# Neighbourhood attention scores: from two stacked full-array products per head to three half-row products for two heads at once

## The chip, the cores and the metric

The kernel runs on one core of one Trainium2 chip. The metric is the device time of one execution in microseconds (us). The core has four engines that compute: TensorE (PE, matrix products into PSUM, with weight loads that overlap the products), VectorE (DVE), ScalarE (ACT) and GpSimd (POOL). SyncE (SP) issues the DMAs. They run side by side, each through its own instructions in order, and wait for one another on semaphores.

## The reference, cut to what matters

One encoder layer over two requests of 2048 tokens with 1024 features. A normalised input is projected; four of the projections (q_b, k_b, v_b, g_b, each 512 wide) feed the second branch, an attention over a grid of 32 rows by 64 columns with 8 heads of 64 features. A token sees a window of 8 rows by 16 columns:

```python
def neighbourhood_attn(q, k, v, rpb):
    ...
    def row(r):
        ...
        kb = kr[:, :, key_cols]
        vb = vr[:, :, key_cols]
        sc = jnp.einsum('bnqhd,banchd->bnhqac', qr, kb).astype(jnp.float32) * scale
        ...
        sc = jnp.where(mask, sc + bias.astype(jnp.float32), -jnp.inf)
        sc = sc.reshape(b, NA_N_COL_BLOCKS, B_HEADS, NA_COL_BLOCK, wr * NA_KEY_COLS)
        pr = jax.nn.softmax(sc, axis=-1)
        ...
        o = jnp.einsum('bnhqac,banchd->bnqhd', pr, vb)
        return o.reshape(b, GRID_W, B_WIDTH)
```

q_b and k_b are normalised per head before this; the branch's output is multiplied by a gate and goes, with that of a first branch (windowed attention), through an output projection. All of it is in 32-bit floats.

## The kernel before, in words

**Precision.** PE's fast 32-bit form keeps fewer digits than a full float. So each operand is split into a high part, which is the value rounded to that form, and a low part, the rest, and a product is made of three: high by high, low by high, high by low. ACT writes the high part (a copy that rounds), DVE or POOL the low part (a subtraction).

**Stages.** A first stage handles the windowed attention, a second the neighbourhood attention, a third the output projection and what follows. In the second stage (loop at the end of `emit`, `f` from 2 x NT to 6 x NT) there are 64 units: two halves of four heads each, two requests, and sixteen blocks of 8 x 16 tokens. A unit is `unit_b(f)`. Its 128 queries meet a window of keys of 288, 360, 384 or 512 columns, by the block's place on the grid (`window`, L31).

**The order on PE is written out by hand.** Each product goes through `mm` (L201) or `tr` (L204, a transpose), and `pinned` (L193) chains them in the order of the program. The generator `stream` yields the projection products of tiles that come up to six units later (`proj_b`, 48 products of 512 columns per unit: `pqk` for queries and keys, `pvg` for values and gate). `PLAN_B` (L83) tells where in a unit's 10320 planned nanoseconds of projection each step of the attention is put in: `sc` (scores), `pt` (transposed weights of the softmax), `po` (product with the values), `fin` (gate and store), `prep` (the next unit's queries). An entry is the place, whether it belongs to this unit (1) or the previous one (0), the step and its index.

**The scores of one head before.** A head has 64 features, and PE has 128 rows. `keys_b` (L598) therefore stacks a head's keys: for the head at rows 0 to 63 of the transposed tile the high part lies in rows 0 to 63 and the low part in rows 64 to 127; for the other head it is the other way round. That takes, for each unit's key tile, four instructions of ACT (L607) and four of DVE (L608), each over 64 partitions. `prep_b` (L671) does the like for the queries: ACT writes the high part to one half (L680), DVE the low part to the same half of a second tile (L681) whose other half is zero, and POOL copies the high part to the other half (L683). With that, a head's scores are two products over all 128 rows (L713): the doubled high query by the stacked keys gives high by high and high by low at once, and the low query by the stacked keys gives low by high.

**After the products** `softmax` (L214, the instruction of L217) has DVE add the bias, take the maximum and free the PSUM buffer. Score buffers, the buffers of `pt` and that of `fin` share one tag, `sc`, with three PSUM buffers in turn (`PSB`, L60).

Of the kernel before, what the change touches and what calls it, by code (L numbers as in the profile page):

```python
# [11 lines left out]
F32 = mybir.dt.float32  # L12
F32R = mybir.dt.float32r
I32 = mybir.dt.int32
AF = mybir.ActivationFunctionType
ALU = mybir.AluOpType
# [22 lines left out]
def row_type(b):  # L39
    return (0, 1, 1, 2)[b]  # L40


def col_type(cb):
    return (0, 1, 1, 2)[cb]


def bias_offsets():
# [33 lines left out]
    (0.75, 1, "pt", 0), (0.79, 1, "pt", 1), (0.88, 1, "pt", 2),  # L81
)
PLAN_B = (  # L83
    (0.00, 1, "sc", 0), (0.03, 1, "sc", 1), (0.07, 1, "sc", 2), (0.09, 0, "po", 2), (0.11, 1, "sc", 3), (0.16, 0, "po", 3),
    (0.24, 0, "fin", 0), (0.35, 1, "prep", 0),
    (0.45, 1, "pt", 0), (0.52, 1, "pt", 1), (0.60, 1, "pt", 2), (0.66, 1, "po", 0), (0.74, 1, "pt", 3), (0.80, 1, "po", 1),
)
# [2 lines left out]
def emit(ctx, tc, io):  # L90
    nc = tc.nc
# [4 lines left out]
    def ptile(shape, tag, name):  # L96
        tag = PSM.get(tag, tag)
        return pp.tile(shape, F32, tag=tag, name=name, bufs=PSB[tag])
# [10 lines left out]
    wk = cp.tile([128, 2], F32, tag="wk", name="wk")  # L109
# [91 lines left out]
    def mm(out, lhsT, rhs, start, stop):  # L201
        pinned(nc.tensor.matmul(out, lhsT, rhs, start=start, stop=stop))  # L202

    def tr(out, in_):  # L204
        pinned(nc.tensor.transpose(out, in_, ident))  # L205
# [8 lines left out]
    def softmax(i, ps, n, bias, sm):  # L214

        s = main.tile([128, 512], F32, tag="s", name="s", bufs=SB)
        nc.vector.tensor_tensor_reduce(out=s[:, :n], in0=ps[:, :n], in1=bias, scale=1.0, scalar=-3.0e38,  # L217
                                       op0=ALU.add, op1=ALU.max, accum_out=sm["mx"][:, i:i + 1])
        sm["s"].append(s)
# [41 lines left out]
    ap = ab_stack.enter_context(tc.tile_pool(name="ab", bufs=1))  # L261
# [55 lines left out]
    def big(shape, dt, name):  # L317
        return ap.tile(shape, dt, tag="big", name=name, bufs=3)
# [38 lines left out]
    for i in range(4):  # L357
        nc.vector.tensor_tensor(out=tab[i // 2][:, i % 2], in0=cs[:, i % 2],
                                in1=rw[:, i].unsqueeze(1).broadcast_to([128, NT, 16]), op=ALU.mult)
# [4 lines left out]
    q2s = []  # L364
# [5 lines left out]
    ks_b, w_b, held = [], {}, {}  # L370
# [227 lines left out]
    def keys_b(kt, b, cb):  # L598
        pkt = ptile([128, 2, 16, 8], "ms", "pktb")
        for i in range(2):  # L600
            tr(pkt[:, i].rearrange("p c r -> p (c r)"), kt[:, 2 * i:2 * i + 2, :].rearrange("p h d -> p (h d)"))
        for i in range(2):
            for e in range(2):
                a, z = 64 * e, 64 - 64 * e
                hi, lo = (ks_b[i][p:p + 64, 8 * b:8 * b + 8, e, 16 * cb:16 * cb + 16].rearrange("p r c -> p c r")
                          for p in (a, z))
                nc.scalar.activation(hi, pkt[a:a + 64, i], AF.Copy, scale=wk[a:a + 64, 1:2])  # L607
                nc.vector.scalar_tensor_tensor(out=lo, in0=pkt[a:a + 64, i], scalar=wk[a:a + 64, 1:2],  # L608
                                               in1=hi.bitcast(F32), op0=ALU.mult, op1=ALU.subtract)

    def proj_b(f):
        half, st = divmod(f - 2 * NT, 2 * NT)
        s, j = divmod(st, NT)
        b, cb = divmod(j, 4)
        if f < 2 * NT + 8:
            regroup_next()
        if not ks_b:
            ks_b.extend(big([128, 32, 2, 64], F32R, f"ks_b{i}") for i in range(2))
        w_qk, w_vg = w_b[half]
        xr = xt.pop(f)  # L620
        pk = ptile([128, 512], "pj", "pqk")
        for i, c in enumerate(project(pk, xr, lambda k, b: ready("wa", k, w_qk)[:, b, :], 215)):
            at = i + 24 if f in last else i
            if i == PD and f == 2 * NT + 9:
                stats_b(1)
            if at in HX:
                split(f + 1, HX[at])
            yield c
        sq = ap.tile([128, 512], F32, tag="sq", name="sqb", bufs=2)
        nc.scalar.activation(sq, pk, AF.Square)  # L630
        ssq = ap.tile([128, 8], F32, tag="ssq", name="ssqb", bufs=3)
        nc.vector.tensor_reduce(out=ssq, in_=sq.rearrange("p (h d) -> p h d", d=HD), op=ALU.add, axis=AX.X)
        vr = ap.tile([128, 8], F32, tag="vr", name="vrb", bufs=2)
        y = ap.tile([128, 8], F32, tag="y", name="yb", bufs=4)
        nc.vector.tensor_scalar(out=vr, in0=ssq, scalar1=1.0 / HD, scalar2=ep_b[:, st:st + 1],
                                op0=ALU.mult, op1=ALU.add)
        rsqrt(ap, vr, y, 8, "rqb")
        qg = ap.tile([128, 2, 4, HD], F32, tag="qg", name="qg", bufs=6)
        kt = ap.tile([128, 4, HD], F32, tag="kt", name="kb", bufs=2)
        for dst, c in ((kt, 4), (qg[:, 0], 0)):  # L640
            nc.vector.tensor_tensor(out=dst, in0=pk[:, 64 * c:64 * c + 256].rearrange("p (h d) -> p h d", d=HD),
                                    in1=y[:, c:c + 4].unsqueeze(2).broadcast_to([128, 4, HD]), op=ALU.mult)
        yield 0, False
        pv = ptile([128, 512], "pj", "pvg")
        for i, c in enumerate(project(pv, xr, lambda k, b: ready("wb", k, w_vg)[:, b, :], 215)):
            if i + 24 in HX and f not in last:
                split(f + 1, HX[i + 24])
            yield c
            if i == (KB if f not in last else 10):
                if f < 2 * NT + 2:  # L650
                    pending.append((kt, b, cb))
                else:
                    keys_b(kt, b, cb)
        v = ap.tile([128, 4, 2, HD], F32R, tag="sq", name="vb", bufs=2)
        vp = pv[:, 0:256].rearrange("p (h d) -> p h d", d=HD)
        nc.scalar.activation(v[:, :, 0, :], vp, AF.Copy, scale=rs_b[:, st:st + 1])
        nc.vector.scalar_tensor_tensor(out=v[:, :, 1, :], in0=vp, scalar=rs_b[:, st:st + 1],
                                       in1=v[:, :, 0, :].bitcast(F32), op0=ALU.mult, op1=ALU.subtract)
        for w, (c0, ncol) in COL_WIN.items():
            lo, hi = max(c0, 16 * cb), min(c0 + ncol, 16 * cb + 16)  # L660
            if lo < hi:
                nc.sync.dma_start(v_d[half, s, w][8 * b:8 * b + 8, lo - c0:hi - c0].rearrange("r c h a d -> c r (h a d)"),
                                  v[8 * (lo - 16 * cb):8 * (hi - 16 * cb)].bitcast(F32).rearrange("p h a d -> p (h a d)"))
        gs = qg[:, 1].rearrange("p h d -> p (h d)")
        nc.scalar.activation(gs, pv[:, 256:512], AF.Tanh, scale=hr_b[:, st:st + 1])
        nc.vector.scalar_tensor_tensor(out=gs, in0=gs, scalar=1.0, in1=pv[:, 256:512], op0=ALU.add, op1=ALU.mult)
        held[f] = qg[:, 0], gs
        next(combining, None)
        yield 0, False

    def prep_b(f):  # L671
        q = held[f][0]
        pqt = ptile([128, 256], "ms", "pqtb")
        for i in range(2):
            tr(pqt[:, 128 * i:128 * i + 128], q[:, 2 * i:2 * i + 2, :].rearrange("p h d -> p (h d)"))
        q1 = ap.tile([128, 2, 256], F32R, tag="q1", name="q1b", bufs=3)
        q1, q2 = [q1[:, e] for e in range(2)], [q2s[f % 2][:, e, :256] for e in range(2)]
        for e in range(2):
            a, z = 64 * e, 64 - 64 * e
            nc.scalar.copy(q1[e][a:a + 64], pqt[a:a + 64])  # L680
            nc.vector.tensor_tensor(out=q2[e][a:a + 64], in0=pqt[a:a + 64], in1=q1[e][a:a + 64].bitcast(F32),  # L681
                                    op=ALU.subtract)
            nc.gpsimd.tensor_copy(q1[e][z:z + 64], q1[e][a:a + 64])  # L683
        return q1, q2

    bt = []

    def unit_b(f):
        half, st = divmod(f - 2 * NT, 2 * NT)
        s, j = divmod(st, NT)  # L690
        b, cb = divmod(j, 4)
        _, gs = held[f]
        r0, nr, c0, ncol, rows = window(b, cb)
        kc, nch = rows * ncol, nr // rows
        n = nr * ncol
        if cb != 2:
            off, _ = BIAS_OFF[(row_type(b), col_type(cb))]
# [4 lines left out]
        bias = bt[-1]  # L702
# [4 lines left out]
                              .rearrange("r c h a d -> (r c) (h a d)"))  # L707
        sm, p_ts, got = sm_tiles(), [], {}

        def sc(h):  # L710
            ps = ptile([128, 512], "sc", "scb")
            for j, q in enumerate(qs[f]):
                mm(ps[:, :n].rearrange("p (r c) -> p r c", c=ncol), q[h % 2][:, 128 * (h // 2):128 * (h // 2) + 128],  # L713
                   ks_b[h // 2][:, r0:r0 + nr, h % 2, c0:c0 + ncol], j == 0, j == 1)
            softmax(h, ps, n, bias[:, h, :n], sm)
            if h == 3:
                next(exps(sm, n, hr_b[:, st:st + 1], gs))

        def pt(x):
# [119 lines left out]
    qs = {}  # L839
# [85 lines left out]
    with tc.tile_pool(name="c", bufs=1) as op:  # L925
# [192 lines left out]
        for m in range(7 * len(groups)):  # L1118
            n, i = divmod(m, 7)
# [104 lines left out]
```

## Time and profile before

| what | us |
|---|---|
| median of 3 runs | 2605.88 |
| lowest and highest of them | 2604.47, 2607.68 |
| the profiled execution's own time | 2603.58 |
| its span, first to last instruction | 2601.7 |
| span of the second stage's scores, first to last product | 852 to 1888 |

The span is 1.9 us shorter than the execution's time; the rest lies around it. A row of a group reads: line of the kernel, engine, operation, tile written <- tiles read, shapes, count | busy time, mean ns of one | idle time of the engine before them, and what ended it. A row of a stretch reads: from : to, length, then busy time and count for PE, PEld (weight loads), DVE, ACT and POOL, the granted clock, the DMA engines' share and GB/s. A row of the waits reads: who waited for whom, us in total, times, longest. A row of the timeline reads: start, length, engine, line, operation, tiles, shapes, count.

### The profile page before, as it was taken

The page shows a single profiled execution, that of the slowest core. Times are in us where ns is not written, and L with a number is a line of the kernel's source. Part 1 is how long each engine was busy: PE and PEld are TensorE (multiplying, and loading weights), DVE is VectorE, ACT ScalarE, POOL GpSimd, SP SyncE. Part 2 cuts the span into 40 slices and gives each one's busy share as a digit, 9 for nine tenths or more (in the row PEclk, how much of TensorE's full clock was granted, in tenths as well). Part 3 has the DMA queues.
Part 4 walks back from the last instruction along what each step waited for, and adds up shares of the span by engine and source line. Part 5 has one row for each costly group of instructions (what it writes and reads, how often), then busy time and mean ns, then how long its engine had stood idle before and what let it go on. Part 6 is the DMA issues. An engine that isn't in the chain of part 4 may idle for free.

```text
span 2601.7 us, 47013 instructions
## 1 busy us (share of the span) xinstructions
PE 2547.1 (98%) x16080; PEld 2269.7 (87%) x16080; DVE 1963.3 (75%) x5702; ACT 1416.3 (54%) x3327; POOL 789.2 (30%) x996
## 2 busy tenths in 40 slices
PE   7999999999999999999999999999989999999999
PEld 6888888888877888888788888887989999999999
DVE  6888988889897788888888888888655648555454
ACT  5666666666675666666766666666432214222222
POOL 3333333333322333333233332321122423233321
PEclk9999999999999999999999999999999999999999
DMA  5333322111143564555654554457575445232221
GB/s 178 108 102 108 101 93 94 54 60 56 58 111 120 174 188 153 185 184 163 225 178 150 187 177 150 153 155 214 172 251 190 150 165 196 82 116 92 78 82 45
DMA packets 227519, 357.51 MB, mean 137 GB/s; under 512 B 37936, under 2 KB 115376, under 8 KB 222128
## 3 DMA queue, kind: packets, MB, share of 16 engines
q1 hardware_dynamic: 227280, 354.50, 42.8%
q8 instruction: 128, 2.10, 0.3%
q14 instruction: 111, 0.91, 0.1%
HBM read 266.33 MB, written 105.92 MB: 143 GB/s over the span
## 4 chain that ended last, share of the span: by engine, by line
PE 87%; DVE 5%; DMA 2%; ACT 2%; issue 2%; POOL 1%; SPq 0%; POOLq 0%; DVEq 0%; ACTq 0%
PE pqk L202 13%; PE pvg L202 12%; PE acca L1034 11%; PE accc L1034 9%; PE pg L202 6%; PE pq L202 5%; PE pob L202 4%; PE pple L202 3%; PE ptb L205 3%; PE scb L202 3%; PE pt L205 3%; PE po L202 3%; PE sc L202 3%; PE pk L202 3%; PE pout L202 3%
## 5 line engine op out<-in xcount | busy, mean ns | idle before, releaser
L232 ACT ACTIVATE s<-s,nm 128x384 f32<-128x384 f32 (+4 forms) x512 | 306.2, 599 | 340.6 <-DVE nm L228 185.0
L202 PE MATMUL pvg<-wb,xr 128*128 128x512 f32 x1536 | 455.2, 404 | 0.0
L202 PE MATMUL pqk<-wa,xr 128*128 128x512 f32 x1536 | 437.4, 407 | 0.0
L295 POOL TENSOR_TENSOR xr<-stx,xr 128x512 fp32r<-128x512 f32 x192 | 247.6, 1297 | 193.4 <-ACT xr L294 189.9
L202 PEld LDWEIGHTS pqk<-wa,xr 128*128 128x128 f32 x1536 | 267.5, 189 | 37.2
L202 PEld LDWEIGHTS pvg<-wb,xr 128*128 128x128 f32 x1536 | 267.4, 189 | 31.3
L202 PE MATMUL pg<-wb,xr 128*128 128x512 f32 x768 | 232.4, 410 | 4.1 <-DVE q L454 4.1
L202 PE MATMUL pq<-wa,xr 128*128 128x512 f32 x768 | 222.8, 404 | 3.6 <-ACT wa L147 2.8
L243 POOL TENSOR_TENSOR g<-qg,rd 128x256 f32<-128x256 f32 x64 | 39.7, 620 | 495.1 <-DVE rd L241 481.3
L1034 PE MATMUL acca<-opd,s 128*128 128x256 f32 x1344 | 164.6, 283 | 2.9 <-ACT r L1066 2.5
L1034 PEld LDWEIGHTS acca<-opd,s 128*128 128x128 f32 x1344 | 162.7, 192 | 3.6 <-ACT r L1066 2.7
L202 PEld LDWEIGHTS pq<-wa,xr 128*128 128x128 f32 x768 | 141.1, 191 | 28.3 <-ACT wa L147 3.4
L217 DVE CUSTOM_DVE_ANT_0 s<-scb,bias 128x288 f32<-128x288 f32 (+3 forms) x256 | 142.0, 555 | 29.1 <-PE scb L202 23.6
L202 PEld LDWEIGHTS pg<-wb,xr 128*128 128x128 f32 x768 | 137.9, 190 | 25.0 <-issue 4.6
L726 ACT CAST p_t<-ptb 96x384 fp32r<-96x384 f32 (+3 forms) x256 | 129.7, 508 | 54.1 <-PE ptb L205 52.3
L727 DVE TENSOR_TENSOR p_t<-ptb,p_t 96x384 fp32r<-96x384 f32 (+3 forms) x256 | 149.0, 584 | 9.1 <-ACT p_t L726 6.4
L607 ACT ACTIVATE ks_b<-pktb,wk 64x128 fp32r<-64x128 f32 x256 | 125.4, 490 | 49.1 <-DVE ks_b L608 40.6
L202 PEld LDWEIGHTS pob<-p_t,vw 128*128 128x128 f32 (+2 forms) x832 | 133.2, 190 | 20.8 <-DVE p_t L727 2.5
L608 DVE SCALAR_TENSOR_TENSOR ks_b<-pktb,wk,ks_b 64x128 fp32r<-64x128 f32 x256 | 115.1, 449 | 39.8 <-ACT ks_b L607 33.4
L202 PE MATMUL pob<-p_t,vw 128*128 128x256 f32 (+2 forms) x832 | 141.0, 283 | 2.0 <-DVE p_t L727 2.0
L1000 POOL TENSOR_TENSOR opd<-sum,opd 128x1024 fp32r<-128x1024 f32 x28 | 69.5, 2484 | 232.6 <-ACT opd L986 232.6
L217 DVE CUSTOM_DVE_ANT_0 s<-sc,mask 128x384 f32<-128x384 f32 (+1 forms) x256 | 135.8, 532 | 0.8
(197 smaller groups left out, 5909.1 us busy)
## 6 DMA issues: line engine op xcount, KB each, us to landing
stx<-x_b SPq DMA_DIRECT2D x128, 256.0 KB
vw<-v_d SPq DMA_DIRECT2D x112, 256.0 KB
stx<-x_a SPq DMA_DIRECT2D x64, 256.0 KB
stn<-x_n SPq DMA_DIRECT2D x64, 256.0 KB
v_d<-vb SPq DMA_DIRECT2D x64, 256.0 KB
x1r<-x_d SPq DMA_DIRECT2D x16, 1024.0 KB
y_t<-r SPq DMA_DIRECT2D x64, 256.0 KB
v_d<-vb SPq DMA_DIRECT2D x96, 128.0 KB
```

Source lines behind the costliest of these rows:

```text
L202: pinned(nc.tensor.matmul(out, lhsT, rhs, start=start, stop=stop))
L205: pinned(nc.tensor.transpose(out, in_, ident))
L217: nc.vector.tensor_tensor_reduce(out=s[:, :n], in0=ps[:, :n], in1=bias, scale=1.0, scalar=-3.0e38, op0=ALU.add, op1=ALU.max, accum_out=sm[ ...
L232: nc.scalar.activation(ss[i][:, :n], ss[i][:, :n], AF.Exp, bias=nm[:, i:i + 1], accum_out=den[:, i:i + 1])
L243: nc.gpsimd.tensor_tensor(out=g2, in0=gs.rearrange("p (h d) -> p h d", h=4), in1=rd.unsqueeze(2).broadcast_to([128, 4, HD]), op=ALU.mult)
L295: nc.gpsimd.tensor_tensor(out=lo, in0=raw, in1=hi.bitcast(F32), op=ALU.subtract)
L607: nc.scalar.activation(hi, pkt[a:a + 64, i], AF.Copy, scale=wk[a:a + 64, 1:2])
L608: nc.vector.scalar_tensor_tensor(out=lo, in0=pkt[a:a + 64, i], scalar=wk[a:a + 64, 1:2], in1=hi.bitcast(F32), op0=ALU.mult, op1=ALU.subtract)
L726: nc.scalar.copy(p_t[:kc, :nch, 0], pf)
L727: nc.vector.tensor_tensor(out=p_t[:kc, :nch, 1], in0=pf, in1=p_t[:kc, :nch, 0].bitcast(F32), op=ALU.subtract)
L1000: each(lambda x, y, z: eng.tensor_tensor(out=x, in0=y, in1=z, op=ALU.subtract), out, a, b)
L1034: pinned(nc.tensor.matmul(ps[:, kk], w[k][:, a, c:c + 128], o[:, b, k], start=i in (0, 1, 4) and kk == 0 and k == 0 and j == 0, stop=k == ...
```

## The change

Keys: `ks_b[0]` now holds the high part and `ks_b[1]` the low part of all four heads, head pair by head pair, each over all 128 partitions, so that a key tile takes two instructions of ACT and two of DVE. Queries: one tile with the high and the low part, one instruction of ACT and one of DVE, no copy on POOL. Scores: `sc(i)` handles heads 2i and 2i + 1 in two score buffers, with three products each. Head 2i uses partitions 0 to 63 of keys and queries, head 2i + 1 partitions 64 to 127, and the six products alternate between the two. The plan has two `sc` entries instead of four, at 0.00 and 0.10, and the previous unit's third `po` moves from 0.09 to 0.06. The products are the same three parts as before: high by high, low by high, high by low.

```diff
 PLAN_B = (
-    (0.00, 1, "sc", 0), (0.03, 1, "sc", 1), (0.07, 1, "sc", 2), (0.09, 0, "po", 2), (0.11, 1, "sc", 3), (0.16, 0, "po", 3),
+    (0.00, 1, "sc", 0), (0.06, 0, "po", 2), (0.10, 1, "sc", 1), (0.16, 0, "po", 3),
     (0.24, 0, "fin", 0), (0.35, 1, "prep", 0),
...
         for i in range(2):
-            for e in range(2):
-                a, z = 64 * e, 64 - 64 * e
-                hi, lo = (ks_b[i][p:p + 64, 8 * b:8 * b + 8, e, 16 * cb:16 * cb + 16].rearrange("p r c -> p c r")
-                          for p in (a, z))
-                nc.scalar.activation(hi, pkt[a:a + 64, i], AF.Copy, scale=wk[a:a + 64, 1:2])
-                nc.vector.scalar_tensor_tensor(out=lo, in0=pkt[a:a + 64, i], scalar=wk[a:a + 64, 1:2],
-                                               in1=hi.bitcast(F32), op0=ALU.mult, op1=ALU.subtract)
+            hi, lo = (k[:, i, 8 * b:8 * b + 8, 16 * cb:16 * cb + 16].rearrange("p r c -> p c r") for k in ks_b)
+            nc.scalar.activation(hi, pkt[:, i], AF.Copy, scale=wk[:, 1:2])
+            nc.vector.scalar_tensor_tensor(out=lo, in0=pkt[:, i], scalar=wk[:, 1:2], in1=hi.bitcast(F32),
+                                           op0=ALU.mult, op1=ALU.subtract)
...
-            ks_b.extend(big([128, 32, 2, 64], F32R, f"ks_b{i}") for i in range(2))
+            ks_b.extend(big([128, 2, 32, 64], F32R, f"ks_b{i}") for i in range(2))
...
-        q1 = ap.tile([128, 2, 256], F32R, tag="q1", name="q1b", bufs=3)
-        q1, q2 = [q1[:, e] for e in range(2)], [q2s[f % 2][:, e, :256] for e in range(2)]
-        for e in range(2):
-            a, z = 64 * e, 64 - 64 * e
-            nc.scalar.copy(q1[e][a:a + 64], pqt[a:a + 64])
-            nc.vector.tensor_tensor(out=q2[e][a:a + 64], in0=pqt[a:a + 64], in1=q1[e][a:a + 64].bitcast(F32),
-                                    op=ALU.subtract)
-            nc.gpsimd.tensor_copy(q1[e][z:z + 64], q1[e][a:a + 64])
-        return q1, q2
+        q = ap.tile([128, 2, 256], F32R, tag="q1", name="q1b", bufs=3)
+        nc.scalar.copy(q[:, 0], pqt)
+        nc.vector.tensor_tensor(out=q[:, 1], in0=pqt, in1=q[:, 0].bitcast(F32), op=ALU.subtract)
+        return q
...
-        def sc(h):
-            ps = ptile([128, 512], "sc", "scb")
-            for j, q in enumerate(qs[f]):
-                mm(ps[:, :n].rearrange("p (r c) -> p r c", c=ncol), q[h % 2][:, 128 * (h // 2):128 * (h // 2) + 128],
-                   ks_b[h // 2][:, r0:r0 + nr, h % 2, c0:c0 + ncol], j == 0, j == 1)
-            softmax(h, ps, n, bias[:, h, :n], sm)
-            if h == 3:
+        def sc(i):
+
+            pss = [ptile([128, 512], "sc", "scb") for _ in range(2)]
+            q = qs[f]
+            for j, (a, b) in enumerate(((0, 0), (1, 0), (0, 1))):
+                for e in range(2):
+                    r = slice(64 * e, 64 * e + 64)
+                    mm(pss[e][:, :n].rearrange("p (r c) -> p r c", c=ncol), q[r, a, 128 * i:128 * i + 128],
+                       ks_b[b][r, i, r0:r0 + nr, c0:c0 + ncol], j == 0, j == 2)
+            for e in range(2):
+                softmax(2 * i + e, pss[e], n, bias[:, 2 * i + e, :n], sm)
+            if i == 1:
                 next(exps(sm, n, hr_b[:, st:st + 1], gs))
```

## The prediction

> **What bounds the kernel now.** I read the first and fourth parts of the page first: what is busy, and which work the end hangs on.
>
> ```profile
> span 2601.7 us, 47013 instructions
> PE 2547.1 (98%) x16080; PEld 2269.7 (87%) x16080; DVE 1963.3 (75%) x5702; ACT 1416.3 (54%) x3327; POOL 789.2 (30%) x996
> ...
> PE 87%; DVE 5%; DMA 2%; ACT 2%; issue 2%; POOL 1%; SPq 0%; POOLq 0%; DVEq 0%; ACTq 0%
> ```
>
> TensorE (PE) is busy nearly all the time and carries 87% of the chain that ends last. The change touches the second attention stage alone, so the second look is the table of stretches for that stage (from the first product of its scores, 852 us, to the last, 1888 us) and the waits of PE within it.
>
> ```profile
> 852.00:1890.00 1038.00, 1026.41 (x5783) 875.75 (x5782) 838.22 (x2559) 664.46 (x1576) 315.40 (x391) 0.99 0.56 176
> ```
>
> ```profile
> PE pout L202 <- DVE o_r L802: 4.5, 3, 3.5
> PE ptb L205 <- ACT s L232: 2.4, 3, 1.0
> PE pob L202 <- DVE p_t L727: 2.0, 1, 2.0
> PE scb L202 <- DVE mx L217: 1.0, 1, 1.0
> PE scb L202 <- ACT qg L665: 1.0, 2, 0.5
> PE pktb L205 <- DVE otb L746: 0.3, 1, 0.3
> ```
>
> Of 1038 us PE is busy in 1026 at a granted clock of 0.99, and all its waits together are 11.2 us. VectorE (DVE) is busy in 838, ScalarE (ACT) in 664, GpSimd (POOL) in 315. In this stage the price of anything is what it does to PE; work taken from the others can win no more than some of those 11.2 us.
>
> **What the scores cost now.** Here are all their products, grouped by width (two kinds: the stacked high part q1b, and the low part q):
>
> ```profile
> L202 PE MATMUL scb<-ks_b,q1b 128*128 128x512 f32 x64 | 25.7, 402 | 2.0 <-DVE mx L217 1.0 <-ACT qg L665 1.0
> L202 PE MATMUL scb<-ks_b,q 128*128 128x512 f32 x64 | 25.5, 399 | 0.0
> ...
> L202 PE MATMUL scb<-ks_b,q 128*128 128x384 f32 x64 | 21.8, 341 | 0.0
> L202 PE MATMUL scb<-ks_b,q1b 128*128 128x384 f32 x64 | 21.7, 340 | 0.0
> L202 PE MATMUL scb<-ks_b,q 128*128 128x360 f32 x64 | 20.9, 326 | 0.0
> L202 PE MATMUL scb<-ks_b,q1b 128*128 128x360 f32 x64 | 20.8, 324 | 0.0
> ...
> L202 PE MATMUL scb<-ks_b,q1b 128*128 128x288 f32 x64 | 19.0, 296 | 0.1
> L202 PE MATMUL scb<-ks_b,q 128*128 128x288 f32 x64 | 18.9, 295 | 0.0
> ```
>
> Their mean durations overlap, so they aren't what a product takes of PE. That is the step from one start to the next, which the timeline gives:
>
> ```profile
> 1409.32 0.34 PE L202 MATMUL scb<-ks_b,q1b 128*128 128x384 f32 x1
> 1409.49 0.34 PE L202 MATMUL scb<-ks_b,q 128*128 128x384 f32 x1
> 1409.67 0.62 PE L202 MATMUL pvg<-wb,xr 128*128 128x512 f32 x2
> 1410.13 0.34 PE L202 MATMUL scb<-ks_b,q1b 128*128 128x384 f32 x1
> ```
>
> Two products of 384 columns take 0.35 us, two of 512 take 0.46 us: 0.458 and 0.449 ns a column. I take 0.455. A width has 128 products, so the scores stream 128 x (512 + 384 + 360 + 288) = 197,632 columns, 89.9 us.
>
> The same rows give the **tail**: the record of a 384-column product is 0.34 us, its step 0.175, so it runs 0.165 us on beside the next product.
>
> **Part 1, three half-row products for a pair of heads instead of four full ones.** A unit (64 of them) had four heads with two products each over 128 rows. Now a call handles two heads with three products each, one head on rows 0 to 63 and the other on rows 64 to 127, issued in turn: 128 calls of six. If the two halves really run together, a call takes three widths where two heads took four: 3/4 of 89.9 is 67.4 us, **-22.5 us**. No row of this trace has a 64-row product, so I bound it from the other side: if they run one after the other, there are six widths for four, 134.9 us, +45.0. I take the pair as concurrent: the halves share no row, weight or PSUM bank.
>
> The Trainium skill, "TensorE: Matmul & The Clock Gate", Part 3, says that matmuls on distinct row groups run concurrently and start about 4 ns apart; no run here shows it yet.
>
> **Part 2, the weight loads.** Loads rise from 8 to 12 a unit, each still 128 columns, two to a slot. How fast may load and product follow each other? The densest rows are transposes and 256-column products:
>
> ```profile
> 1403.54 0.49 PE L205 MATMUL ptb<-ident,s 128*128 128x128 f32 x3
> 1403.79 0.94 PE L202 MATMUL pqk<-wa,xr 128*128 128x512 f32 x3
> 1404.56 0.52 PE L202 MATMUL pob<-p_t,vw 128*128 128x256 f32 x3
> 1404.92 0.40 PE L202 MATMUL pqk<-wa,xr 128*128 128x512 f32 x1
> ```
>
> Three transposes and three 512-column products take 1.02 us; less 3 x 0.23 that is 0.11 for a transpose with its load. Three 256-column ones take 0.36, 0.12 each. Ends: the loads are hidden (0), or each couple of load and product costs its 0.11 and a slot can't be under 0.22. In the latter case 96 slots each of 384, 360 and 288 take 0.22 and 96 of 512 take 0.233: 85.7 us, and of the gain 4 us are left. I take 0: the loads of the 288-column products in the list above, step 0.13, leave no gap.
>
> **Part 3, changing between whole rows and half rows.** Every other product of the stage uses the whole array, so each call changes over and back: 256 changes. The low end is 0: in the rows just quoted transposes and products alternate, and the sum leaves nothing for it; nor do products with fewer rows show a gap:
>
> ```profile
> L202 PE MATMUL pob<-p_t,vw 96*128 96x256 f32 x192 | 32.9, 280 | 0.0
> ```
>
> But all of these start at row 0, one at a time. The new ones start at rows 0 and 64 and leave the array side by side. If the array has to empty first, the tail of the product before, 0.165 us, is no longer beside the next one; if the next weights may not be loaded meanwhile either, 0.11 comes on top, 0.275. I take 0.165, because the nearest thing to a half-row product waiting for the array is a product whose tail lies beside nothing: 256 x 0.165 = **+42.2 us**. Ends 0 and 70.4. The break-even is 22.5 / 256 = 0.088 us a change.
>
> The Trainium skill, "TensorEngine Tiling (Array Packing)", Key Properties, states that changing the tiling mode, not just the tile, drains the engine. It gives no price; by it the upper half of this interval is the place to look, and the trace, which has no such change, neither agrees nor disagrees.
>
> **Part 4, the splits.** Keys:
>
> ```profile
> L607 ACT ACTIVATE ks_b<-pktb,wk 64x128 fp32r<-64x128 f32 x256 | 125.4, 490 | 49.1 <-DVE ks_b L608 40.6
> ...
> L608 DVE SCALAR_TENSOR_TENSOR ks_b<-pktb,wk,ks_b 64x128 fp32r<-64x128 f32 x256 | 115.1, 449 | 39.8 <-ACT ks_b L607 33.4
> ```
>
> and queries:
>
> ```profile
> L680 ACT CAST q1b<-pqtb x128: 346/368/372, 801.0 to 1879.1; 64x256 fp32r<-64x256 f32 x128
> L683 POOL CAST q1b<-q1b x128: 392/394/801, 801.7 to 1879.8; 64x256 fp32r<-64x256 f32 x128
> L681 DVE TENSOR_TENSOR q<-pqtb,q1b x128: 405/422/431, 801.9 to 1880.3; 64x256 fp32r<-64x256 f32 x128
> ```
>
> Each pair over 64 partitions becomes one over 128 with as many elements a partition, so I give it the same duration. ACT loses 128 x 0.490 + 64 x 0.368 = 86 us, DVE 128 x 0.449 + 64 x 0.422 = 84 us, POOL its 128 copies of 0.394, 50 us. None of them is on the path: the six waits above name neither line. Gain 0, at most the waits on DVE and ACT, 6.7 us without `pout`. If a full-height split were twice as long, the engines would be where they are now: 0 too. No DMA is added or moved.
>
> **Part 5, order and buffers.** Heads 0 and 1 now come at the unit's start, heads 2 and 3 at 0.10 of it (1032 planned ns), with the previous unit's third `po` between, at 0.06. The three score buffers must now give two at once; the fourth head takes the buffer of the first, as before. It is free when DVE has read it:
>
> ```profile
> 1409.87 0.56 DVE L217 CUSTOM_DVE_ANT_0 s<-scb,bias 128x384 f32<-128x384 f32 x1
> ...
> 1410.36 0.68 DVE L632 TENSOR_REDUCE ssqb<-sqb 128x8 f32<-128x512 f32 x1
> ```
>
> From the product's end (1409.67) that is 0.76 us, or 1.44 with the 0.68 us reduction ahead of it. Between the calls PE has five projection products and a `po` of three: 5 x 0.23 + 0.36 = 1.5 us. So it just fits: 0. If another instruction like that reduction comes ahead, the second call waits 0.62 us, and with it everything on PE, since its order is fixed: 64 x 0.62 = 40 us.
>
> **Sum.** -22.5 + 42.2 = +19.7 us on the profiled execution's own 2603.6 us, 2623.3; the median of the runs shown is 2.3 above that execution, so 2625.6, **2625**.
>
> **The rivals.**
> - **The changes cost nothing** (not slower). Same pairs, loads hidden, but the array passes from whole to half rows as it passes from transposes to products. Then the gain of part 1 stands: 2606 - 22.5 = 2583. For it: no gap in any row above. Against: none of them starts at row 64. It decides below 0.088 us a change; where it holds in part (0.02 us), 2588.
> - **The loads bind.** No price for the change, but slots of 0.22 to 0.235: 2602 to 2606, within 0.2%.
> - **The halves don't run together**: six widths for four, +45, 2651 (with a price for changes still more). The change would then not do what it says. For it: every product in the trace streams alone.
> - **The buffer is late**: pairs gain 22.5, the second call waits 40: 2623. Against: 1.5 us of cover for 1.44.
>
> **How the numbers follow.** Chances: forecast 0.37 (its own range 2611 to 2653, with 0.11 to 0.275 a change), free changes 0.33, loads 0.12, no concurrency 0.13, late buffer 0.05. 0.2%, 5 us, is about what a measurement of this kernel can tell from no change. Faster: 0.33 and a quarter of the loads' case, 0.36. Same: the rest of that case and a sliver of the forecast with a price near break-even, 0.11. Slower: 0.53. Cases of both signs hold most of the chance, so the range goes from 2581 (free changes and some of the waits) to 2651 (no concurrency, and nearly the forecast's upper end); outside lie half of the case without concurrency and edges, under 0.2.
>
> **What the profile after would show.** Part 1: a pair's two starts some ns apart and its next pair one width later, against starts a width apart if they run alone. Part 2: slots of 288 and 512 columns with different steps, or all at 0.22. Part 3: the first pair starting one step after the projection product before it, or 0.165 us and more later, and the same again for the product behind the last pair. Part 4: ACT, DVE and POOL lower by 86, 84 and 50 us, with PE's list of waits hardly changed. Part 5: a wait of `scb` for DVE's `mx`, 64 times or hardly ever. The forecast is wrong if a change costs under 0.088 us while the halves run together, and also if the scores take more than 110 us although no step stretches at a change.

## The result, and the profile after

The changed kernel takes 2628.11 us in the median of 4 runs (2622.40 to 2629.25), the kernel before 2605.61: the ratio is 1.0081, with a 95% interval of 1.0064 to 1.0099. On a second chip it is 1.0066 (1.0054 to 1.0079), 2621.03 against 2603.24. The change makes the kernel slower by 18 to 22 us. 2625 had been forecast. On the first chip its runs lie 7 us apart, so a few us of this are chance.

The span and the busy times of the engines, from the page of the kernel after:

```profile
span 2627.3 us, 46780 instructions
...
PE 2574.4 (98%) x16336; PEld 2237.8 (85%) x16336; DVE 1863.4 (71%) x5510; ACT 1311.5 (50%) x3135; POOL 739.5 (28%) x868
```

ACT, DVE and POOL are relieved of 105, 100 and 50 us, and PE is longer by 27, about the 25.6 us that the span grew. The scores now run from 855 to 1914 us, 1059 us instead of 1036: 22.8 us more. The other 3 us lie ahead of the first score product (855.4 us, before 852.4; on the second chip 850.5), so the change didn't make them. The second stage in the table of stretches:

```profile
852.00:1890.00 1038.00, 1029.24 (x5835) 820.47 (x5834) 728.61 (x2340) 557.63 (x1372) 267.52 (x265) 0.99 0.56 173
```

and PE's waits in it:

```profile
PE pob L202 <- DVE p_t L724: 3.2, 1, 3.2
PE pvg L202 <- ACT wb L147: 2.5, 1, 2.5
PE pout L202 <- DVE o_r L799: 2.0, 1, 2.0
PE pout L202 <- ACT o_r L798: 0.9, 1, 0.9
```

The listed waits are fewer than before, 8.6 us against 11.2, and no `scb` is among them. So the loss isn't a wait for another engine. It lies in PE's own steps. The score products in groups:

```profile
L202 PE MATMUL scb<-ks_b,q1b 64*128 64x512 f32 x192 | 31.8, 431 | 0.1
L202 PE MATMUL scb<-ks_b,q1b 64*128 64x384 f32 x192 | 25.6, 372 | 0.0
L202 PE MATMUL scb<-ks_b,q1b 64*128 64x360 f32 x192 | 24.3, 357 | 0.0
L202 PE MATMUL scb<-ks_b,q1b 64*128 64x288 f32 x192 | 21.2, 325 | 0.0
```

There are 768 half-row products, as the change says. How they follow one another shows in PE's timeline around one call of 384 columns:

```profile
1349.23 0.52 PE L202 MATMUL pob<-p_t,vw 96*128 96x256 f32 x3
1349.59 0.63 PE L202 MATMUL pvg<-wb,xr 128*128 128x512 f32 x2
1350.14 0.80 PE L202 MATMUL scb<-ks_b,q1b 64*128 64x384 f32 x6
1350.87 0.96 PE L202 MATMUL pvg<-wb,xr 128*128 128x512 f32 x3
1351.67 0.40 PE L202 MATMUL pob<-p_t,vw 96*128 96x256 f32 x2
```

and, with the window set around the first and the last pair alone:

```profile
1350.14 0.44 PE L202 MATMUL scb<-ks_b,q1b 64*128 64x384 f32 x2
...
1350.60 0.34 PE L202 MATMUL scb<-ks_b,q1b 64*128 64x384 f32 x2
```

The weight loads (PEld) around the same call, and the load of one score product of before:

```profile
1350.14 0.47 PEld L202 LDWEIGHTS scb<-ks_b,q1b 64*128 64x128 f32 x6 [0.36 <-DVE vrb L632]
1350.87 0.53 PEld L202 LDWEIGHTS pvg<-wb,xr 128*128 128x128 f32 x3 [0.26 <-issue]
```

```profile
1409.09 0.19 PEld L202 LDWEIGHTS scb<-ks_b,q1b 128*128 128x128 f32 x1
```

Before, the load began 0.23 us ahead of its product (1409.32), beside the product in front. At a change it begins together with its product, at 1350.14 and 1350.87, and the loader has stood idle until then. The name of DVE in the first row is no cause: every call has the same delay, and the second row names no engine.

Read the products against the steps of before, 0.23 us for 512 columns and 0.175 for 384.
- Six products take 0.73 us (1350.14 to 1350.87). Six widths would be 1.05: the pairs do run together, three widths are 0.525.
- Ahead of them two projection products take 0.55 us and not 0.46: **0.09 us of delay, which I read as the array emptying.**
- The first two slots take 0.46 and not 0.35, and the first record is 0.44 and not 0.34: **0.105 us for a weight load that nothing covers.**
- The last slot takes 0.27 and not 0.175: the same delay again, 0.09.
- The three projection products behind take 0.80 and not 0.69: the second uncovered load, 0.11.

Together 0.39 to 0.40 us for the two changes of a call, just under 0.20 each, where a call gains one width, 0.13 to 0.235 us. The trace shows the delays and the late loads; it doesn't show the emptying itself. The record of the product ahead, whose end is modelled, runs to 1350.22, 0.08 us past the start of the pair, so it isn't the whole tail that the pair waits for.

The time from the product ahead of a call to the second one behind it, less the usual step of the two neighbours, is in the median 0.79, 0.89, 0.93 and 1.10 us for the four widths, before 0.53, 0.65, 0.72 and 0.94 for two heads. Over all calls that is 118.4 us of PE, before 90.9: **+27.5**. With the few calls that hold a wait it is 119.3 against 94.2. The stage grew by 22.8 only, so some 5 us came back elsewhere in it, 2.6 of them as shorter listed waits; the rest isn't traced.

### The profile page after: what moved, and what is told of

Same layout as the page of the kernel before. It is cut to its first block, busy times and chain, and to the rows that moved or that the text cites. A ratio compares the mean times of both kernels' runs of the same rounds, so it can differ in the third digit from the quotient of the medians.

```text
span 2627.3 us, 46780 instructions
## 1 busy us (share of the span) xinstructions
PE 2574.4 (98%) x16336; PEld 2237.8 (85%) x16336; DVE 1863.4 (71%) x5510; ACT 1311.5 (50%) x3135; POOL 739.5 (28%) x868
## 5 line engine op out<-in xcount | busy, mean ns | idle before, releaser
L202 PEld LDWEIGHTS pvg<-wb,xr 128*128 128x128 f32 x1536 | 259.7, 189 | 63.2 <-issue 28.4
L750 POOL TENSOR_TENSOR o_tb<-otb 128x256 f32<-128x256 f32 x64 | 48.7, 761 | 616.9 <-issue 397.7
L742 ACT COPY otb<-pob 64x512 f32<-64x512 f32 x128 | 74.2, 580 | 278.0 <-PE pob L202 277.9
L205 PE MATMUL ptb<-ident,s 128*128 128x128 f32 (+2 forms) x832 | 133.5, 274 | 0.0
```

What stands on the lines that cost most here:

```text
L742: nc.scalar.copy(ot[a:a + 64], pq[z:z + 64])
L750: nc.gpsimd.tensor_tensor(out=o_t.rearrange("p i (r c) -> p i c r", c=16), in0=got["ot"][:, :, 0].rearrange("p i (c r) -> p i c r", r=8), ...
```

## The experiments

**Half as many changes.** Both calls of a unit stand back to back; the fourth score buffer is borrowed from the projections.

```diff
-    (0.00, 1, "sc", 0), (0.06, 0, "po", 2), (0.10, 1, "sc", 1), (0.16, 0, "po", 3),
+    (0.00, 1, "sc", 0), (0.00, 1, "sc", 1), (0.06, 0, "po", 2), (0.16, 0, "po", 3),
...
-            pss = [ptile([128, 512], "sc", "scb") for _ in range(2)]
+            pss = [ptile([128, 512], "pj" if i and e else "sc", "scb") for e in range(2)]
```

> The changed kernel with both score calls of a unit back to back at 0.00 of the unit, twelve half-row products in one block; the fourth score buffer is borrowed from the projections' three. Changes between whole and half rows: 128 instead of 256. Theory 1 (each change costs about 0.195 us: 0.09 for the array to empty, 0.105 for a weight load that nothing covers): 128 x 0.195 = 25 us less than the changed kernel, about 2603. Theory 2 (the loss comes from half-row products that are slow in themselves): no change, 2628. Theory 3 (it comes from the order of the steps and the buffers): slower than 2628, since one projection buffer is gone and four heads come at once.

Measured: 2605.86, ratio to before 1.0013 (1.0003 to 1.0022). PE's timeline around one block of twelve:

```profile
1347.39 2.25 PE L202 MATMUL pqk<-wa,xr 128*128 128x512 f32 x9
1349.58 1.33 PE L202 MATMUL scb<-ks_b,q1b 64*128 64x384 f32 x12
1350.84 0.96 PE L202 MATMUL pvg<-wb,xr 128*128 128x512 f32 x3
1351.64 0.52 PE L202 MATMUL pob<-p_t,vw 128*128 128x256 f32 x3
```

Nine projection products take 2.19 us and not 2.10, the block 1.26 and not 6 x 0.175 = 1.05, the three behind it 0.80 and not 0.69: 0.41 us in all, for twelve products as for six. The price belongs to the change, not to the product. By the median block the scores of all units take 93.2 us, 25.2 less than in the changed kernel, as forecast (with waits 95.7, 23.6 less). The kernel lies 3 us over its kernel before, where the changed kernel lay 18 to 22 over its own: the time fell by 15 to 19 us and not by 25, because PE waits more, 15.8 us in all against 8.6. The four longest:

```profile
PE pvg L202 <- ACT wb L147: 3.4, 1, 3.4
PE pout L202 <- DVE o_r L799: 3.1, 3, 2.4
PE pvg L202 <- DVE qg L663: 2.3, 2, 1.2
PE pktb L205 <- DVE otb L743: 2.2, 1, 2.2
```

The third of these is the lent buffer.

In a block of 288 columns the slots are no longer than a width either:

```profile
1109.34 1.06 PE L202 MATMUL scb<-ks_b,q1b 64*128 64x288 f32 x12
1110.33 0.96 PE L202 MATMUL pvg<-wb,xr 128*128 128x512 f32 x3
```

Six slots take 0.99 us; less the 0.20 of the load and the delay in them, that is 0.13 each.

**The price by itself.** The kernel before gets one short product ahead of each head's two, whose result the head's first product overwrites: once over rows 0 to 63, as a control over all 128, and later over rows 0 to 31.

```diff
             ps = ptile([128, 512], "sc", "scb")
+            mm(ps[:, :64].rearrange("p (r c) -> p r c", c=16), qs[f][0][h % 2][:64, 128 * (h // 2):128 * (h // 2) + 128],
+               ks_b[h // 2][:64, r0:r0 + 4, h % 2, c0:c0 + 16], True, True)
             for j, q in enumerate(qs[f]):
```

> The kernel before with one more product ahead of each head's two: 64 columns wide, over rows 0 to 63 alone, into the same score buffer, which the head's own first product then overwrites. It adds 256 short products and 512 changes between whole and half rows. Theory 1 (0.09 us for the array to empty and 0.105 us for an uncovered weight load at each change): 512 x 0.195 + 256 x 0.03 = 108 us, about 2713. Rival (a change costs no more than any further product of that size): as the kernel with the short product over all 128 rows, 15 to 30 us over 2605.

> The kernel before with the same short product of 64 columns ahead of each head's two, but over all 128 rows: no change between whole and half rows. Both theories: 256 x 0.06 to 0.11 us, 15 to 28 us over 2605. It is the control of the kernel with the half-row product; the difference of the two, over 512, is the price of a change.

Measured with 64 rows 2704.24, ratio 1.0389 (1.0373 to 1.0404); with 128 rows 2629.21, 1.0101 (1.0084 to 1.0118). The timeline of the kernel with half rows, heads of 288 columns:

```profile
1357.10 0.62 PE L202 MATMUL scb<-ks_b,q1b 64*128 64x64 f32 x2
1357.56 0.29 PE L202 MATMUL scb<-ks_b,q 128*128 128x288 f32 x1
1357.69 0.61 PE L202 MATMUL pvg<-wb,xr 128*128 128x512 f32 x2
1358.24 0.62 PE L202 MATMUL scb<-ks_b,q1b 64*128 64x64 f32 x2
```

(the row of two holds the short product and the head's first), and that of the control:

```profile
1101.63 0.41 PE L202 MATMUL scb<-ks_b,q1b 128*128 128x64 f32 x2
1101.88 0.30 PE L202 MATMUL scb<-ks_b,q 128*128 128x288 f32 x1
1102.01 0.62 PE L202 MATMUL pvg<-wb,xr 128*128 128x512 f32 x2
1102.47 0.41 PE L202 MATMUL scb<-ks_b,q1b 128*128 128x64 f32 x2
```

From one short product to the next it is 1.14 us with half rows, 0.84 with whole rows, and a head's two products and two projections without one are 0.46 + 2 x 0.133 = 0.73. So the whole-row product costs 0.11 us (the couple of a load and a narrow product), the half-row one 0.41, of which its 64 columns are 0.03. Two changes are 0.38, as in the changed kernel. Over the runs it is 100.7 / 256 = 0.393 us against 25.6 / 256 = 0.100. My 108 us came out as 101. The difference of the two runs over 512 changes, which I had called the price of a change, is only 0.147 us. It is too low as I read the rows: the control's own 0.10 is a load that its narrow product doesn't cover, and in the half-row kernel the uncovered load is part of the change.

> The kernel before with a short product of 64 columns ahead of each head's two, over rows 0 to 31 alone. With rows 0 to 63 it took 2704, with all rows 2629; a product over 96 rows showed no step of its own in the kernel before. Theory 1 (any change of the division of the rows empties the array and uncovers a load, whatever the division): as with 64 rows, 2704 within 5 us. Rival (the price falls with the share of the array that the product uses): 2650 to 2690.

Measured: 2705.96, ratio 1.0391 (1.0377 to 1.0405), as with 64 rows. Between 32 and 64 rows the share of the array that the product uses doesn't matter; that the division changes does. Products over 96 and 120 rows, which the kernel before has, aren't a change in this sense: they stand among full ones at the same step, 0.12 us for 256 columns (three over 96 rows take 0.36 in the timeline above).

**The order within a call.** Three products of one head, then three of the other.

```diff
-            for j, (a, b) in enumerate(((0, 0), (1, 0), (0, 1))):
-                for e in range(2):
+            for e in range(2):
+                for j, (a, b) in enumerate(((0, 0), (1, 0), (0, 1))):
```

> The changed kernel with the six products of a call in another order: three of one head, then three of the other. Theory 1 (a pair runs at the same time because its two products stand next to each other): only the last of the first head and the first of the second can overlap, five widths instead of three, 128 x 2 x 0.176 = 45 us more, about 2673; six widths, 67 us more, if not even these. Theory 2 (half-row products of the two halves don't help each other, the order doesn't matter): 2628.

Measured: 2633.77, ratio 1.0118 (1.0103 to 1.0133); neither 2673 nor 2628. The timeline in a window of 20 ns around the start of a call:

```profile
1348.01 0.39 PE L202 MATMUL pvg<-wb,xr 128*128 128x512 f32 x1
1348.32 0.45 PE L202 MATMUL scb<-ks_b,q1b 64*128 64x384 f32 x2
```

Two products have started within the window's 20 ns: the second half begins 10 ns after the first, although its head stands behind three products of the other in the program. Two products of one head can't be meant, since those follow one another a width apart. In this trace each half of the array follows its own products. Both theories were wrong about the mechanism: the halves help each other, and the order doesn't matter for that. In all calls the scores take 120.3 us, 1 more than with alternating heads. What the rest of the 6 us was had to be asked on one chip.

**The order of the steps and the buffers.** The kernel before with its stacked full-row products, but with two heads in a call and the changed kernel's plan.

```diff
-        def sc(h):
-            ps = ptile([128, 512], "sc", "scb")
...
+        def sc(i):
+            pss = [ptile([128, 512], "sc", "scb") for _ in range(2)]
+            for j, q in enumerate(qs[f]):
+                for e in range(2):
+                    mm(pss[e][:, :n].rearrange("p (r c) -> p r c", c=ncol), q[e][:, 128 * i:128 * i + 128],
+                       ks_b[i][:, r0:r0 + nr, e, c0:c0 + ncol], j == 0, j == 1)
```

> The kernel before, with its stacked operands and two full products per head, but in the changed kernel's order: heads 0 and 1 in one call at 0.00, heads 2 and 3 in one call at 0.10, the previous unit's third product with the values at 0.06, two score buffers taken at once. Theory 1 (order and buffers cost nothing): the time of before, 2605 within 3 us. Theory 3 (the order of the steps and the buffers make the loss): up to 2628.

Measured: 2605.32, ratio 1.0012 (1.0003 to 1.0021), 2.6 us. PE's waits for the score buffers in it:

```profile
PE scb L202 <- DVE mx L217: 2.1, 2, 1.4
...
PE scb L202 <- ACT qg L665: 1.6, 2, 0.8
```

Four waits in 128 calls: two buffers at once nearly always come free in time. The order makes about a tenth of the loss, by the interval at most a quarter (0.8 to 5.5 us).

**The splits.** The changed kernel with as many splits on ACT and DVE as before, each over 64 partitions (the queries alike).

```diff
-            nc.scalar.activation(hi, pkt[:, i], AF.Copy, scale=wk[:, 1:2])
-            nc.vector.scalar_tensor_tensor(out=lo, in0=pkt[:, i], scalar=wk[:, 1:2], in1=hi.bitcast(F32),
-                                           op0=ALU.mult, op1=ALU.subtract)
+            for a in (0, 64):
+                r = slice(a, a + 64)
+                nc.scalar.activation(hi[r], pkt[r, i], AF.Copy, scale=wk[r, 1:2])
+                nc.vector.scalar_tensor_tensor(out=lo[r], in0=pkt[r, i], scalar=wk[r, 1:2], in1=hi[r].bitcast(F32),
+                                               op0=ALU.mult, op1=ALU.subtract)
```

> The changed kernel with the splits of keys and queries in halves of 64 partitions again, as many instructions on ScalarE and VectorE as before the change (only GpSimd's copies stay away). Theory 1 (what the splits save lies beside TensorE's work): 2628 within 3 us, with ScalarE's and VectorE's busy time about 85 us higher each. Rival (the relief of ScalarE and VectorE gives back part of the loss): 5 to 15 us slower than 2628.

Measured: 2633.42, ratio 1.0113 (1.0098 to 1.0128). From 852 to 1890 us ACT and DVE are busy 81 and 80 us more, as meant. Since 5 us more was the rival's answer, and the first chip of the changed kernel another one, three kernels ran again on one chip.

> The changed kernel once more, on the chip on which the next two run, so that the small differences between them can be told. Its ratio to the kernel before, first 1.0081: 1.006 to 1.011.

> The changed kernel with three products of one head, then three of the other. Its trace has the second head start 10 ns behind the first and not five widths, and its blocks of scores take 120.3 us of TensorE against 119.3. Theory (the order within a call doesn't matter, each half follows its own products): within 3 us of the changed kernel on this chip. Rival (the 5 us by which its first time lay above come from the order): 4 to 7 us above.

> The changed kernel with the splits in halves of 64 partitions. Theory 1 (the splits lie beside TensorE's work): within 3 us of the changed kernel on this chip. Rival (the relief of ScalarE and VectorE gives back some of the loss): 5 to 10 us above, as its first time suggested.

Measured there: the changed kernel 2621.03, heads in turn 2632.61 (1.0110; 1.0095 to 1.0126), half splits 2631.85 (1.0106; 1.0092 to 1.0120). Both lie about 11 us above, more than either rival had said (4 to 7 and 5 to 10). Where? In the changed kernel on this chip, PE's waits in the second stage are

```profile
PE pob L202 <- DVE p_t L724: 2.7, 1, 2.7
PE pvg L202 <- ACT wb L147: 2.5, 1, 2.5
PE pout L202 <- DVE o_r L799: 2.0, 1, 2.0
```

with half splits

```profile
PE pob L202 <- DVE q1b L679: 6.2, 1, 6.2
PE pout L202 <- DVE o_r L803: 3.4, 2, 3.0
```

and with heads in turn

```profile
PE pob L202 <- DVE p_t L724: 3.3, 1, 3.3
PE pktb L205 <- DVE otb L743: 3.1, 12, 0.3
```

The biggest, on `pob`, are single events at the change from the first four heads to the last four, near 1280 us, where ACT and DVE split sixteen tiles of new weights beside their usual work. The timeline of half splits there:

```profile
1280.28 3.12 DVE L148 SCALAR_TENSOR_TENSOR wa<-wa,nw 128x512 fp32r<-128x512 f32 x3
...
1283.33 0.41 DVE L679 TENSOR_TENSOR q1b<-pqtb,q1b 64x256 fp32r<-64x256 f32 x1
1283.66 0.67 DVE L728 TENSOR_TENSOR p_t<-ptb,p_t 128x512 fp32r<-128x512 f32 x1
...
1285.19 1.23 PE L202 MATMUL pob<-p_t,vw 128*128 128x256 f32 x4 [6.19 <-DVE q1b L679]
```

DVE makes three weight splits, then the queries' and then the transposed weights of the softmax for which PE stands. And the clock is lower afterwards. Stretches of 5 us (PE's busy time first, the granted clock behind the five engines) in half splits

```profile
1280.00:1285.00 5.00, 0.00 (x0) 0.00 (x0) 4.97 (x8) 2.65 (x6) 1.41 (x2) 0.80 0.87 293
1285.00:1290.00 5.00, 4.81 (x16) 4.08 (x17) 3.78 (x9) 2.58 (x6) 1.13 (x1) 0.52 0.41 126
```

and in the changed kernel on the same chip

```profile
1275.00:1280.00 5.00, 2.32 (x13) 1.71 (x12) 4.48 (x9) 4.34 (x11) 2.29 (x3) 0.90 0.89 277
1280.00:1285.00 5.00, 5.00 (x24) 4.16 (x24) 3.45 (x7) 2.63 (x6) 1.10 (x1) 0.76 0.66 203
```

In the first stretch of half splits PE makes no product, so its lower clock costs nothing; in the second it costs 5 x 0.48 = 2.4 us. In the changed kernel, after 2.7 us of waiting, the second stretch costs 5 x 0.24 = 1.2. The Trainium skill, "TensorE: Matmul & The Clock Gate", Part 1, says that an idle window of about 3.4 us puts the clock to half; here it was lower after a wait of 6.2 us and also after one of 2.7, which is shorter than that window. All waits listed for half splits come to 14.9 us, those of the changed kernel on this chip to 8.3; with the clock that is 8 of the 10.6 us between their spans (2630.0 and 2619.4). For heads in turn the waits are 12.9 us and the clock loses some 4; about 5 of the 12.7 us between the spans stay open, 2 of them behind the last score, and why DVE's `otb` is late there twelve times wasn't tried.

So in the steady units the splits stay hidden, as the forecast had it: the list of half splits names no wait for keys or queries but the one near 1280 us, and that one is longer than the changed kernel's. That the relief is worth 11 us there isn't shown: heads in turn, which has the changed kernel's splits, lies as far above, and the kernel before, with as many half-height splits, waits 5.4 us between 1250 and 1350 us, the changed kernel 5.7. How long PE stands at that place depends on more than the number of splits.

The changed kernel itself differs by 7 us between two chips. Of the 7.9 us between the two profiled spans 4.9 lie ahead of the first score (855.4 against 850.5 us) and 3.2 between the first and the last. There the first profile has a clock of 0.50 from 1285 to 1290 us and of 0.74 from 1305 to 1310, behind waits of 3.2 and 2.5 us; on the second chip the wait of 2.5 us left the clock at 1.00. The scores take 119.3 us in the one and 119.4 in the other.

None of these kernels beats the kernel before. Of those with half-row products, one block per unit comes nearest; for windows of 512 columns it gains two widths, 0.47 us, for 0.39, for narrower ones it loses.

## Why the prediction was right

- **Part 1 (-22.5 us, pairs run together): right.** Slots of the steady kind, as between the twelve products of a block, are one width.
- **Part 2 (loads hidden within a call): right.** Slots of 288 columns would be 0.22 us otherwise, and in a block of twelve they are 0.13; six slots of 384 took 1.26 us with both price parts in them, 0.175 each without.
- **Part 3 (+42.2 us): the mechanism right, the size somewhat low, its make-up wrong.** I had taken the whole tail of a product, 0.165 us, and no load. It is 0.09 of delay, well under the tail, and 0.105 for the load, which I had put at the far end: 0.195 to 0.20 a change, 50 us. With the gain of part 1 that is +27.4, measured +27.5. "Every other product of the stage uses the whole array" wasn't so: `pob` has products over 96 and 120 rows, which cost no change.
- **Part 4 (splits, 0): right in the steady units, open in one place.** Full-height splits take as long as half-height ones (0.493 and 0.446 us for the keys against 0.490 and 0.449):

```profile
L604 ACT ACTIVATE ks_b<-pktb,wk 128x128 fp32r<-128x128 f32 x116 | 57.1, 493 | 6.4 <-DVE ks_b L605 3.1 <-PE pktb L205 2.9
L605 DVE SCALAR_TENSOR_TENSOR ks_b<-pktb,wk,ks_b 128x128 fp32r<-128x128 f32 x117 | 52.2, 446 | 0.6 <-ACT ks_b L604 0.6
```

  Keys and queries together fell by 87 us on ACT and 85 on DVE, as forecast; why the engines' busy time fell by 105 and 100 isn't shown. With half-height splits the kernel took 5 us more on another chip and 11 on the same one, about 5 of these at the change of the weights, but how much of that is the relief stays open. I had bounded the gain by the waits, 6.7 us, without the clock that follows a wait.
- **The sum: near by luck.** The price was some 8 us too small, and what else PE loses in the stage, which I had left unchanged, fell: the stage grew by 5 us less than its scores, on the second chip by 8 (1055.8 us, +19.6). The two nearly cancel, so 2625 was nearer than its parts; and 3 us of the first chip's difference lie ahead of the stage.
- **Part 5 (order and buffers, 0): 2.6 us** by the stacked pairs; it just fits, as worked out, but not always.
- **The rivals.** Free changes: out, 0.20 us against a break-even of 0.088. Loads that bind: out. No concurrency: out. A late buffer: out in the changed kernel, no `scb` waits (on the second chip one of 0.2 us). The Trainium skill, "TensorEngine Tiling (Array Packing)", Key Properties, says that a change of tiling mode drains the engine; the trace agrees in kind, with 0.09 us of delay at each change, and a late load on top.

## What to carry to other kernels

Running two products of 64 rows side by side works, but count the changes, not the products: going over and back cost 0.39 us here, as much as 860 columns of products at 0.455 ns, and a block has to save more than that. If half-row products are wanted, put all of them in one block. And when a kernel is bound by one engine, look at the others where their work bunches up (here at the change of the weights), not in the average: the changed kernel and heads in turn, which differ in the order of products alone, were 11 us apart on one chip, some 4 of them there.

## What the runs showed that was not expected

- The two halves of the array don't keep the order of the program between them: with three products of the first half in front, the second half's first product began 10 ns after the first half's. The Trainium skill, "TensorE: Matmul & The Clock Gate", Part 3, has the products in strict order of the program; across halves this trace shows otherwise, and the trace decides.
- The uncovered load takes 0.105 us for 128 columns. The Trainium skill, "TensorE: Matmul & The Clock Gate", LDWEIGHTS, gives columns / 1.2 ns, 0.107 us, whatever the number of rows; the trace agrees, with 0.105 us ahead of the half-row products and 0.11 ahead of the full ones behind them.
- A product of 64 rows and one of 32 rows among full ones cost the same, 2704.24 and 2705.96 us, while products over 96 and 120 rows keep the step of full ones, 0.12 us for 256 columns.
